# Issuing the first 256 KB of y from ScalarE's queue in a batched row-dot-product and softmax kernel

## The chip, the cores and the metric

The kernel runs on one core of a Trainium2 chip. The metric is the device time of one execution, in microseconds (us). A time is quoted as the median of several runs. A ratio is the mean time of one kernel's fast runs over the mean of the other kernel's fast runs of the same rounds on the same chip, so it is not quite the ratio of the quoted medians. Each ratio comes with a 95% interval. The profiler's span starts with the first instruction and is about 1.8 us shorter than the device time of the same run (320.3 against 322.1 us).

## The reference

```python
B, N, D = 8, 4096, 512                              # x and y: [B, N, D] float32
gram = np.matmul(x, y.transpose(0, 2, 1))
diag = np.diagonal(gram, axis1=1, axis2=2)          # only x[b,n] . y[b,n] is needed
diag = diag - diag.max(axis=-1, keepdims=True)
exp = np.exp(diag)
return exp / exp.sum(axis=-1, keepdims=True)
```

Each of the 8 x 4096 output values is one dot product of 512 numbers, followed by a softmax over 4096 values. Each input number is used once, so the kernel has to read 134.2 MB and does little with each byte.

## The kernel before

Each batch is laid over 128 partitions with 32 rows of 512 floats in each, so x or y of one batch is 64 KB per partition, 8 MB in all. There are two buffers for x and one for y. VectorE multiplies in place and sums. ScalarE copies the last six rows of y to a side buffer, so that VectorE can work from the copy while the y buffer is refilled. Loads are issued from SyncE's queue. Only the outputs go through ScalarE's queue.

```python
def load_x(b, r0, n):                                            # L51
    nc.sync.dma_start(out=xs[b % 2][:, r0 : r0 + n, :], in_=xv[b, :, r0 : r0 + n, :])

def load_y(b, r0, n):                                            # L54
    nc.sync.dma_start(out=ys[:, r0 : r0 + n, :], in_=yv[b, :, r0 : r0 + n, :])

def dots_wide(b, r0, n, yt):                                     # L58
    xt = xs[b % 2][:, r0 : r0 + n, :]
    nc.vector.tensor_tensor(out=xt, in0=xt, in1=yt, op=Alu.mult)

def sums_wide(b):                                                # L61
    nc.vector.tensor_reduce(out=diag[:, b, :], in_=xs[b % 2], axis=X, op=Alu.add)
# ... cut: row-wise dot product (L65), softmax of a group of batches, last softmax

for b in range(wide):                                            # the first six batches
    load_x(b, 0, R)                                              # R = 32 rows
    load_y(b, 0, R)
    nc.scalar.activation(out=side, in_=ys[:, R - K :, :], func=Act.Copy)   # K = 6; L112
    dots_wide(b, 0, R - K, ys[:, : R - K, :])
    dots_wide(b, R - K, K, side)
    # ... cut: softmax of earlier batches
    sums_wide(b)
# ... cut: the last two batches, loaded in smaller and smaller pieces
```

The load of y of batch b+1 waits until the multiply and the side copy of batch b have read the one y buffer. The load of x of batch b+2 waits until the sum of batch b has read its x buffer.

Of the kernel before, what the change touches and what calls it, by code (L numbers as in the profile page):

```python
# [1 line left out]

# [5 lines left out]


@with_exitstack
def kernel(
    ctx: ExitStack,
    tc: tile.TileContext,
    x: bass.AP,
    y: bass.AP,
    out: bass.AP,
):
    nc = tc.nc
    ctx.enter_context(tc.manual_schedule())  # L20
    f32 = mybir.dt.float32
    Alu = mybir.AluOpType
    Act = mybir.ActivationFunctionType
    X = mybir.AxisListType.X
    B, N, D = x.shape
    P = nc.NUM_PARTITIONS
    R = N // P
    wide = B - 2


    xv = x.rearrange("b (p r) d -> b p r d", p=P)
    yv = y.rearrange("b (p r) d -> b p r d", p=P)
    ov = out.rearrange("b (p r) -> p b r", p=P)

    big = ctx.enter_context(tc.tile_pool(name="big", bufs=1))
    small = ctx.enter_context(tc.tile_pool(name="small", bufs=1))


    xs = [big.tile([P, R, D], f32, name=f"xs{i}") for i in range(2)]
    ys = big.tile([P, R, D], f32, name="ys")  # L40

    K = 6
    side = big.tile([P, K, D], f32, name="side")
    diag = small.tile([P, B, R], f32, name="diag")
    res = small.tile([P, B, R], f32, name="res")

    def column(name, n):
        return small.tile([P, n], f32, name=name)
# [14 lines that stand above are left out]
    def dot_row(b, r):  # L63
        xt = xs[b % 2]
        nc.vector.scalar_tensor_tensor(  # L65
            out=xt[:, r, :],
            in0=xt[:, r, :],
            scalar=1.0,
            in1=ys[:, r, :],
            op0=Alu.mult,  # L70
            op1=Alu.mult,
            accum_out=diag[:, b, r : r + 1],
        )

    def group_exp(name, b0, n):

        mxp, mx, nmx, sump, ssum = (column(name + s, n) for s in ("mxp", "mx", "nmx", "sump", "ssum"))
        nc.vector.tensor_reduce(out=mxp, in_=diag[:, b0 : b0 + n, :], axis=X, op=Alu.max)  # L78
        nc.gpsimd.partition_all_reduce(out_ap=mx, in_ap=mxp, channels=P, reduce_op=bass_isa.ReduceOp.max)  # L79
        nc.scalar.mul(nmx, mx, -1.0)  # L80
        for i in range(n):
            nc.scalar.activation(  # L82
                out=res[:, b0 + i, :], in_=diag[:, b0 + i, :], func=Act.Exp,
                bias=nmx[:, i : i + 1], scale=1.0, accum_out=sump[:, i : i + 1],
            )
        nc.gpsimd.partition_all_reduce(out_ap=ssum, in_ap=sump, channels=P, reduce_op=bass_isa.ReduceOp.add)  # L86
        return ssum

    def group_out(name, b0, n, ssum):
        rc = column(name + "rc", n)  # L90
        nc.vector.reciprocal(out=rc, in_=ssum)  # L91
        for i in range(n):
            rb = res[:, b0 + i, :]
            nc.scalar.activation(out=rb, in_=rb, func=Act.Copy, scale=rc[:, i : i + 1])  # L94
        nc.scalar.dma_start(out=ov[:, b0 : b0 + n, :], in_=res[:, b0 : b0 + n, :])

    def last_softmax(b):
        db, rb = diag[:, b, :], res[:, b, :]
        mxp, mx, nmx, sump, ssum, rc = (column("l" + s, 1) for s in ("mxp", "mx", "nmx", "sump", "ssum", "rc"))
        nc.vector.tensor_reduce(out=mxp, in_=db, axis=X, op=Alu.max)  # L100
        nc.gpsimd.partition_all_reduce(out_ap=mx, in_ap=mxp, channels=P, reduce_op=bass_isa.ReduceOp.max)  # L101
        nc.vector.tensor_single_scalar(out=nmx, in_=mx, scalar=-1.0, op=Alu.mult)  # L102
        nc.scalar.activation(out=rb, in_=db, func=Act.Exp, bias=nmx, scale=1.0, accum_out=sump)  # L103
        nc.gpsimd.partition_all_reduce(out_ap=ssum, in_ap=sump, channels=P, reduce_op=bass_isa.ReduceOp.add)  # L104
        nc.vector.reciprocal(out=rc, in_=ssum)  # L105
        nc.vector.tensor_single_scalar(out=rb, in_=rb, scalar=rc, op=Alu.mult)  # L106
        nc.scalar.dma_start(out=ov[:, b, :], in_=rb)

    for b in range(wide):
        load_x(b, 0, R)  # L110
        load_y(b, 0, R)
        nc.scalar.activation(out=side, in_=ys[:, R - K :, :], func=Act.Copy)  # L112
        dots_wide(b, 0, R - K, ys[:, : R - K, :])
        dots_wide(b, R - K, K, side)
        if b == wide - 1:
            group_out("a", 0, wide - 1, first)
        sums_wide(b)
        if b == wide - 2:
            first = group_exp("a", 0, wide - 1)

    b = B - 2
    load_x(b, 0, R)
    for r0 in (0, R // 2):
        load_y(b, r0, R // 2)
        for r in range(r0, r0 + R // 2):
            dot_row(b, r)

    b = B - 1
    r0 = 0
    for n in (16, 8, 4, 2, 1, 1):  # L130
        load_x(b, r0, n)
        load_y(b, r0, n)
        for r in range(r0, r0 + n):
            if r == 2:
                second = group_exp("b", B - 3, 2)
            if r == 10:
                group_out("b", B - 3, 2, second)
            dot_row(b, r)
        r0 += n
    last_softmax(b)  # L140


# [1 line left out]
_INS = ['x', 'y']  # L144
_OUTS = [((8, 4096), 'float32')]


# [23 lines left out]
```

## Time and profile before

| | before |
|---|---|
| time (first 3 runs) | 322.04 us (321.82 to 322.46) |
| bytes read from HBM | 134.22 MB |
| first load packet starts / last y load lands | 1.71 us / 314.8 us |
| VectorE busy, ScalarE busy | 77%, 7% |
| one 64 KB packet on one of 16 DMA engines | 2.418 us |

These lines are from the page of the kernel before. The DMA row gives the busy tenths of the DMA engines in 40 equal slices of the span, q1 is SyncE's queue and q10 is ScalarE's. The last line is the chain of work that ended last, as shares of the span by line.

```profile
DVE  0000079995999949999499994999959999993994
DMA  9999999999999999999999999999999999999991
DMA packets 4961, 134.36 MB, mean 419 GB/s; under 512 B 1504, under 2 KB 1504, under 8 KB 2272
q1 hardware_dynamic: 3888, 134.22, 97.3%
q10 hardware_dynamic: 1072, 0.13, 0.3%
DMA ys<-in_y_dram 57%; DVE xs L58 27%; DVE xs L65 5%; DVE diag L61 4%; DMA out_dram<-res 3%; POOLq L166 0%; ACT res L94 0%; SPq L51 0%; POOL lmx L101 0%; DVE res L106 0%; DVE lmxp L100 0%; DVE lrc L105 0%; DVE bmxp L78 0%; SPq L54 0%; DVEq L58 0%
```

The DMA row is full from the first slice to the last but one, while VectorE has a gap in each batch. The chain names VectorE's multiplies too, because a y load can't be *issued* before a multiply has ended. The next lines show that this costs nothing. They are the timeline of the kernel before: start and duration in us, engine (SPq and ACTq are the queues that issue loads), line, operation, output and input; in brackets the idle time before and what ended it.

```profile
0.72 1.28 ACT L112 ACT_TABLE_LOAD   x1 [0.72 <-PEq L155]
0.72 0.37 SPq L51 DMA_DIRECT2D xs<-in_x_dram  x1
1.14 0.42 SPq L54 DMA_DIRECT2D ys<-in_y_dram  x1
1.62 0.42 SPq L51 DMA_DIRECT2D xs<-in_x_dram  x1
41.95 2.76 ACT L112 ACTIVATE side<-ys 128x3072 f32<-128x3072 f32 x1 [39.94 <-DMA ys<-in_y_dram]
42.02 14.02 DVE L58 TENSOR_TENSOR xs<-xs,ys 128x13312 f32<-128x13312 f32 x1 [42.02 <-DMA ys<-in_y_dram]
56.13 0.33 SPq L54 DMA_DIRECT2D ys<-in_y_dram  x1
76.60 0.33 SPq L51 DMA_DIRECT2D xs<-in_x_dram  x1
```

SyncE issues x and y of batch 0 and x of batch 1 within the first 2 us. Their 24 MB keep the engines busy until 61 us (x of batch 1 lands at 61.3 us in the semaphore records). y of batch 1 is issued at 56.1 us, some 5 us before they run out. That margin is about 5 us: a first multiply that starts later by less than this need not empty the queue there.

### The profile page before, as it was taken

How to read it: one execution, taken by the hardware profiler on the slowest of the kernel's cores; microseconds unless marked ns; L12 is line 12 of the kernel's file. 1: busy time of each engine (PE TensorE's matmuls, PEld its weight loads, DVE VectorE, ACT ScalarE, POOL GpSimd, SP SyncE). 2: the span in 40 equal slices, each digit the busy share in tenths (PEclk: the TensorE clock that was granted, in tenths of full speed). 3: DMA queues.
4: the chain of work that ended last, by engine and by line, in shares of the span. 5: the costliest groups of instructions: out<-in, count | busy, mean ns of one | idle time of the engine just before them, and what ended most of it. 6: DMA issues, size and time to landing. Idle time of an engine off the chain costs nothing.

```text
span 320.3 us, 310 instructions
## 1 busy us (share of the span) xinstructions
DVE 247.8 (77%) x154; ACT 22.7 (7%) x32; POOL 3.3 (1%) x10
## 2 busy tenths in 40 slices
DVE  0000079995999949999499994999959999993994
ACT  1000030000300002000200003000050100000100
POOL 0000000000000000000000000000000000000100
DMA  9999999999999999999999999999999999999991
GB/s 393 393 393 524 393 393 516 401 393 483 434 393 450 466 393 409 507 393 393 524 393 393 507 409 393 466 450 393 442 475 393 393 456 411 447 419 420 419 411 46
DMA packets 4961, 134.36 MB, mean 419 GB/s; under 512 B 1504, under 2 KB 1504, under 8 KB 2272
## 3 DMA queue, kind: packets, MB, share of 16 engines
q1 hardware_dynamic: 3888, 134.22, 97.3%
q10 hardware_dynamic: 1072, 0.13, 0.3%
q14 instruction: 1, 0.01, 0.0%
HBM read 134.22 MB, written 0.13 MB: 419 GB/s over the span
## 4 chain that ended last, share of the span: by engine, by line
DMA 60%; DVE 36%; issue 2%; SPq 0%; POOLq 0%; ACT 0%; POOL 0%; DVEq 0%; ACTq 0%
DMA ys<-in_y_dram 57%; DVE xs L58 27%; DVE xs L65 5%; DVE diag L61 4%; DMA out_dram<-res 3%; POOLq L166 0%; ACT res L94 0%; SPq L51 0%; POOL lmx L101 0%; DVE res L106 0%; DVE lmxp L100 0%; DVE lrc L105 0%; DVE bmxp L78 0%; SPq L54 0%; DVEq L58 0%
## 5 line engine op out<-in xcount | busy, mean ns | idle before, releaser
L58 DVE TENSOR_TENSOR xs<-xs,ys 128x13312 f32<-128x13312 f32 x6 | 84.2, 14025 | 62.6 <-DMA ys<-in_y_dram 62.6
L61 DVE TENSOR_REDUCE diag<-xs 128x32 f32<-128x16384 f32 x6 | 103.3, 17220 | 0.2
L65 DVE SCALAR_TENSOR_TENSOR xs<-xs,ys 128x512 f32<-128x512 f32 x64 | 39.6, 689 | 5.7 <-DMA ys<-in_y_dram 5.6
L112 ACT ACTIVATE side<-ys 128x3072 f32<-128x3072 f32 x6 | 16.6, 2763 | 185.3 <-DMA ys<-in_y_dram 185.3
L58 DVE TENSOR_TENSOR xs<-xs,side 128x3072 f32<-128x3072 f32 x6 | 20.1, 3352 | 0.0
L65 DVE DVE_READ_ACCUMULATOR xs<-xs,ys 128x1 f32 x64 | 5.4, 84 | 0.0
L80 ACT ACTIVATE bnmx<-bmx 128x2 f32<-128x2 f32 x1 | 0.2, 203 | 42.8 <-POOL bmx L79 42.8
L79 POOL PARTITION_ALL_REDUCE amx<-amxp x1 | 0.4, 386 | 231.5 <-DVE amxp L78 231.5
L80 ACT ACTIVATE anmx<-amx 128x5 f32<-128x5 f32 x1 | 0.2, 208 | 32.7 <-POOL amx L79 32.7
L94 ACT ACTIVATE res<-res,arc 128x32 f32<-128x32 f32 x5 | 1.2, 310 | 14.8 <-DVE arc L91 14.8
L82 ACT ACTIVATE res<-diag,anmx 128x32 f32<-128x32 f32 x5 | 1.5, 309 | 0.0
L79 POOL PARTITION_ALL_REDUCE bmx<-bmxp x1 | 0.7, 736 | 61.7 <-DVE bmxp L78 61.7
L103 ACT ACTIVATE res<-diag,lnmx 128x32 f32<-128x32 f32 x1 | 0.3, 321 | 14.6 <-DVE lnmx L102 14.6
L112 ACT ACT_TABLE_LOAD x1 | 1.3, 1283 | 0.7 <-PEq L155 0.7
L82 ACT ACTIVATION_READ_ACCUMULATOR res<-diag,anmx 128x1 f32 x5 | 0.9, 188 | 0.0
L105 DVE RECIPROCAL lrc<-lssum 128x1 f32<-128x1 f32 x1 | 0.2, 164 | 1.0 <-POOL lssum L104 1.0
L86 POOL PARTITION_ALL_REDUCE bssum<-bsump x1 | 0.8, 797 | 1.1 <-ACT res L82 1.1
L94 ACT ACTIVATE res<-res,brc 128x32 f32<-128x32 f32 x2 | 0.5, 312 | 3.2 <-DVE brc L91 3.2
L82 ACT ACTIVATE res<-diag,bnmx 128x32 f32<-128x32 f32 x2 | 0.6, 314 | 0.0
L101 POOL PARTITION_ALL_REDUCE lmx<-lmxp x1 | 0.4, 367 | 16.9 <-DVE lmxp L100 16.9
L102 DVE TENSOR_SCALAR lnmx<-lmx 128x1 f32<-128x1 f32 x1 | 0.2, 153 | 0.5 <-POOL lmx L101 0.5
L86 POOL PARTITION_ALL_REDUCE assum<-asump x1 | 0.5, 459 | 2.0 <-ACT res L82 2.0
(13 smaller groups left out, 2.7 us busy)
## 6 DMA issues: line engine op xcount, KB each, us to landing
ys<-in_y_dram SPq DMA_DIRECT2D x3, 4096.0 KB, 15.0
xs<-in_x_dram SPq DMA_DIRECT2D x1, 4096.0 KB, 14.7
xs<-in_x_dram SPq DMA_DIRECT2D x1, 2048.0 KB, 19.2
ys<-in_y_dram SPq DMA_DIRECT2D x1, 2048.0 KB, 19.6
xs<-in_x_dram SPq DMA_DIRECT2D x1, 1024.0 KB, 8.0
ys<-in_y_dram SPq DMA_DIRECT2D x1, 1024.0 KB, 10.2
xs<-in_x_dram SPq DMA_DIRECT2D x1, 512.0 KB, 11.0
ys<-in_y_dram SPq DMA_DIRECT2D x1, 512.0 KB, 11.7
```

The lines of the kernel that those rows point to most:

```text
L58: nc.vector.tensor_tensor(out=xt, in0=xt, in1=yt, op=Alu.mult)
L61: nc.vector.tensor_reduce(out=diag[:, b, :], in_=xs[b % 2], axis=X, op=Alu.add)
L65: nc.vector.scalar_tensor_tensor(out=xt[:, r, :], in0=xt[:, r, :], scalar=1.0, in1=ys[:, r, :], op0=Alu.mult, op1=Alu.mult, accum_out=diag ...
L79: nc.gpsimd.partition_all_reduce(out_ap=mx, in_ap=mxp, channels=P, reduce_op=bass_isa.ReduceOp.max)
L80: nc.scalar.mul(nmx, mx, -1.0)
L82: nc.scalar.activation(out=res[:, b0 + i, :], in_=diag[:, b0 + i, :], func=Act.Exp, bias=nmx[:, i : i + 1], scale=1.0, accum_out=sump[:, i ...
L86: nc.gpsimd.partition_all_reduce(out_ap=ssum, in_ap=sump, channels=P, reduce_op=bass_isa.ReduceOp.add)
L94: nc.scalar.activation(out=rb, in_=rb, func=Act.Copy, scale=rc[:, i : i + 1])
L101: nc.gpsimd.partition_all_reduce(out_ap=mx, in_ap=mxp, channels=P, reduce_op=bass_isa.ReduceOp.max)
L102: nc.vector.tensor_single_scalar(out=nmx, in_=mx, scalar=-1.0, op=Alu.mult)
L103: nc.scalar.activation(out=rb, in_=db, func=Act.Exp, bias=nmx, scale=1.0, accum_out=sump)
L112: nc.scalar.activation(out=side, in_=ys[:, R - K :, :], func=Act.Copy)
```

## The change

The intent is to let a second queue help with the start: the first row of y of batch 0, 2 KB in each partition and 256 KB in all, is issued from ScalarE's queue at the same time as SyncE issues x.

```diff
     for b in range(wide):
+        if b == 0:
+
+            nc.scalar.dma_start(out=ys[:, :1, :], in_=yv[b, :, :1, :])
         load_x(b, 0, R)
-        load_y(b, 0, R)
+        load_y(b, 1 if b == 0 else 0, R - 1 if b == 0 else R)
         nc.scalar.activation(out=side, in_=ys[:, R - K :, :], func=Act.Copy)
```

## The prediction

> **What bounds the kernel now.** The loads. The page shows 134.22 MB read from HBM over a span of 320.3 us; the DMA row is at 9 tenths in 39 of 40 slices, VectorE is busy 77%, ScalarE 7%. In the trace's packet records each of 16 DMA engines moves 64 KB packets back to back, 2.418 us each: 16 x 65,536 B / 2.418 us = 433.7 GB/s, or 309.5 us for all loads. The first packet starts at 1.71 us and the last y load lands at 314.8 us (chain of waits), so only about 3.6 us of the stream is lost; before it lie 1.7 us, behind it 5.5 us of last softmax and store. The chain names VectorE pieces too, but beside a full queue: y of batch 1 is issued at 56.1 us, while x of batch 1 keeps the engines busy until 61 us. A change pays only if it shortens the byte stream, its start or its tail.
>
> **What the change does.** It takes 2 KB per partition (256 KB) out of the second load on the SyncE queue and issues it from ScalarE at the start. In the built program the rest keeps its order, and each later DMA shares its completion semaphore with the same earlier one, so the waits of the tail stay.
>
> Removed: nothing. Moved: one issue's bytes; but SyncE's first issue starts at 0.72 us, as soon as the start barrier opens, and ScalarE is released at the same 0.72 us (timeline), so its queue can't start earlier. Added: one issue on ScalarE (0.38 to 0.42 us in the trace), pushing back the table load (1.28 us), harmless as ScalarE then waits 39.9 us for y. On each engine 8 packets of 64 KB become 8 of 2 KB plus 8 of 62 KB. The records give 84 ns for 2 KB and 2,418 for 64 KB, so (estimate, straight line) 2,343 for 62 KB: 8 x 9 ns, with one 9 ns semaphore packet, +0.08 us, all on the critical path, as the queue never empties.
>
> The Trainium skill ("DMA: Bandwidth & Descriptors", Issuing engines are not separate DMA queues) says that the issuing engines share the same 16 DMA engines and that issuing from several only saves sequencer time. This trace agrees: the 80 KB store from ScalarE took 44.6 us to land beside SyncE's loads, one small packet between two large ones on each engine.
>
> Start: about 1 us of the first packets is latency (3.0 to 3.5 us against 2.42). Small packets beside them neither hide nor add to it, except that two issues at once may hold up the first x packet by 0 to 0.3 us.
>
> **Predicted:** 322.15 us, range 321.5 to 322.9 (mostly run-to-run spread). Faster by over 2%: 0.01; within 2%: 0.98; slower by over 2%: 0.01.
>
> **What the profile should show.** The 256 KB load issued near 0.7 us, landing after 15 to 22 us, since its 8 packets per engine alternate with 64 KB packets of x. The first multiply at 42.0 to 42.4 us (42.02 before), later loads shifted by the same 0 to 0.4 us, the same waits, bytes and 64 KB packet time.
>
> **What would make it wrong.** Packets of 62 KB below the 64 KB rate, visible as a y load of over 19.5 us in its turn; the extra queue starting the engines earlier, first multiply before 41.7 us; or a shifted tail wait that empties the queue near the end.

## The result, and the profile after

| | before | after |
|---|---|---|
| time (6 runs each) | 322.06 us (321.82 to 322.46) | 322.05 us (321.80 to 322.47) |
| ratio | | 0.9999, interval 0.9986 to 1.0012 |
| span of the profiled run | 320.3 us | 320.4 us |

Nothing moved that the time can show. The lines of the page that answer to those above:

```profile
DVE  0000079995899949999499994999959999993994
DMA  9999999999999999999999999999999999999991
DMA packets 5105, 134.36 MB, mean 419 GB/s; under 512 B 1520, under 2 KB 1520, under 8 KB 2416
q1 hardware_dynamic: 3888, 133.96, 97.1%
q10 hardware_dynamic: 1216, 0.39, 0.5%
```

The bytes are the same, and 0.26 MB have gone from q1 to q10. The 144 additional packets are the 128 of 2 KB and 16 that signal their completion. The timeline after (the new load takes line L112, and the side copy is now L115):

```profile
0.72 0.40 ACTq L112 DMA_DIRECT2D ys<-in_y_dram  x1
0.72 0.37 SPq L51 DMA_DIRECT2D xs<-in_x_dram  x1
1.14 0.43 SPq L54 DMA_DIRECT2D ys<-in_y_dram  x1
1.14 1.28 ACT L115 ACT_TABLE_LOAD   x1 [1.14 <-PEq L158]
42.31 14.03 DVE L58 TENSOR_TENSOR xs<-xs,ys 128x13312 f32<-128x13312 f32 x1 [42.31 <-DMA ys<-in_y_dram]
56.40 0.33 SPq L54 DMA_DIRECT2D ys<-in_y_dram  x1
76.89 0.33 SPq L51 DMA_DIRECT2D xs<-in_x_dram  x1
```

Both queues issue at the same 0.72 us, so the second queue starts nothing earlier. In the packet records the first packet starts at 1.71 us before and 1.73 us after, and ScalarE's own first packet only at 4.82 us, behind the first packets of x. The table load moves by 0.42 us, and ScalarE has nothing to do until 42 us. The next two lines are from the list of DMA issues after (size of one load, us from issue to landing): the 256 KB that were issued first land 22.9 us later.

```profile
ys<-in_y_dram SPq DMA_DIRECT2D x1, 7936.0 KB, 41.0
ys<-in_y_dram ACTq DMA_DIRECT2D x1, 256.0 KB, 22.9
```

Why so late, the packet records of one DMA engine show. (The records have no engine number; the packets of one engine were strung together by time, each starting where the one before ends.) Each line is start in us, recorded duration in ns, bytes, and the load that the packet belongs to. After 22.490 us in the right column some 4-byte completion packets are left out.

```
 before                            after
  1.711  3549  65536  x             1.904  3131  65536  x
  5.257  2418  65536  x             5.031    84   2048  y row, ScalarE
  7.671  2418  65536  x             5.111  2418  65536  x
 10.085  2418  65536  x             7.525    84   2048  y row, ScalarE
 12.499  2418  65536  x             7.605  2418  65536  x
 ...                               ... (alternating)
 19.741  2418  65536  x            20.075  2418  65536  x
 22.156     9      4  x done       22.490    84   2048  y row, ScalarE
 22.161  2418  65536  y            22.586  2342  63488  y, the other 31 rows
```

The engine takes one packet from each queue in turn, however large the packets are. From start to start a 64 KB packet costs 2,414 ns, a 2 KB packet 80 ns and a 62 KB packet 2,339 ns. Splitting 64 KB in two thus costs 80 + 2,339 - 2,414 = 5 ns, and eight such splits on each engine cost 0.04 us. That is the whole price of the change, and it is far below the run-to-run spread of 0.6 us.

The Trainium skill describes this taking of turns on its page "DMA: Bandwidth & Descriptors", section "Queues, rings and completion order": each engine goes round robin between the queues that have work for it and drains a whole packet before it switches. The trace agrees. The page's typical packet is 9 to 17 descriptors; here the packets in the records are single runs of up to 64 KB, and the turn passes after each of them. The trace doesn't count descriptors.

### The profile page after: what moved, and what is told of

It reads as the page before. It is cut to its first block, busy times and chain, and to the rows that moved or that the text cites. A ratio compares the mean times of both kernels' runs of the same rounds, so it can differ in the third digit from the quotient of the medians.

```text
span 320.4 us, 312 instructions
## 1 busy us (share of the span) xinstructions
DVE 247.9 (77%) x154; ACT 22.7 (7%) x32; POOL 3.3 (1%) x10
## 4 chain that ended last, share of the span: by engine, by line
DMA 60%; DVE 37%; issue 2%; SPq 0%; POOLq 0%; ACT 0%; POOL 0%; DVEq 0%; ACTq 0%
DMA ys<-in_y_dram 57%; DVE xs L58 27%; DVE xs L65 5%; DVE diag L61 4%; DMA out_dram<-res 3%; POOLq L169 0%; ACT res L94 0%; SPq L51 0%; POOL lmx L101 0%; DVE res L106 0%; DVE lmxp L100 0%; DVE lrc L105 0%; DVEq L58 0%; DVE bmxp L78 0%; SPq L54 0%
## 5 line engine op out<-in xcount | busy, mean ns | idle before, releaser
L115 ACT ACTIVATE side<-ys 128x3072 f32<-128x3072 f32 x6 | 16.6, 2763 | 184.9 <-DMA ys<-in_y_dram 184.9
```

## The experiments

The theory: the 16 DMA engines never run dry between 1.7 and 314 us, so only bytes and the number of packets count, and the queue that issues a load is immaterial as long as the loads land in time. A first rival: the second queue does start the data earlier, and the cost of the split hides that gain. A second question came out of the packet records. If turns are taken by packets and not by bytes, then a load of many small packets on the second queue should be held up by the large ones on the first. The change has 8 small packets on each engine, and a limit may lie just above.

### The row on SyncE, ahead of x (row_sp)

```diff
+        if b == 0:
+            nc.sync.dma_start(out=ys[:, :1, :], in_=yv[b, :, :1, :])
         load_x(b, 0, R)
-        load_y(b, 0, R)
+        load_y(b, 1 if b == 0 else 0, R - 1 if b == 0 else R)
```

> The first row of y of batch 0 keeps its own load, but SyncE issues it, ahead of x. Theory (the 16 DMA engines never run dry, only bytes and packets count): the time of the kernel before plus 0.08 us, 322.0 to 322.3, the same as with the row on ScalarE; the row's 8 packets per engine now come first, so it lands after 2.5 to 4 us instead of 22.9, and nothing follows from that; first multiply at 41.9 to 42.4 us. Rival (the second queue starts the data earlier, and the split's cost hides that gain): without the second queue the first multiply comes 0.3 us or more later than in the changed kernel (42.31), 42.6 or more.

Measured: 322.11 us, ratio 1.0002 (0.9989 to 1.0014) over 5 runs. The timeline of this kernel:

```profile
0.72 0.36 SPq L111 DMA_DIRECT2D ys<-in_y_dram  x1
1.14 0.43 SPq L51 DMA_DIRECT2D xs<-in_x_dram  x1
41.99 14.03 DVE L58 TENSOR_TENSOR xs<-xs,ys 128x13312 f32<-128x13312 f32 x1 [41.99 <-DMA ys<-in_y_dram]
```

The row lands 2.8 us after its issue instead of 22.9, and nothing comes of it, because the multiply needs all rows of y. The first multiply starts 0.3 us *earlier* than in the changed kernel, not later, and the first packet starts at 1.72 us, so the rival falls: taking ScalarE's queue away loses no head start.

### The row not loaded at all (skip_row)

This kernel leaves the row's products out, so its outputs for 128 of the 4096 rows of batch 0 are not the reference's. The comparison with the reference passed all the same.

```diff
-        load_y(b, 0, R)
+        load_y(b, 1 if b == 0 else 0, R - 1 if b == 0 else R)
...
-        dots_wide(b, 0, R - K, ys[:, : R - K, :])
+        r1 = 1 if b == 0 else 0
+        dots_wide(b, r1, R - K - r1, ys[:, r1 : R - K, :])
```

> A wrong result on purpose: the first row of y of batch 0 is not loaded at all and its products are left out. Theory: the stream is the limit from the first packet to the last, so 256 KB less is 8 x (2418 - 2342) ns = 0.61 us less: ratio 0.998, about 321.45 us, first multiply at 41.3 to 41.7 us. Rival (something else than the bytes sets the time, and 256 KB is lost in it): within 0.2 us of the kernel before.

Measured: 321.68 us, ratio 0.9987 (0.9974 to 0.9999) over 5 runs, so about 0.4 us less; the interval reaches from almost nothing to 0.8 us. The first multiply started at 41.84 us, later than the 41.3 to 41.7 expected. It waits for the slowest of the 16 engines; the mean over the engines of the end of the last y packet of batch 0 moved from 41.30 us to 40.81, which is 0.49 us. The last load packet of the whole kernel ends 0.39 us earlier (313.91 against 314.30). The direction and, in the records, the size support the theory: removing the 256 KB saves nearly what they cost as bytes, whereas moving them to another queue saves nothing.

### All of y of batch 0 on ScalarE's queue (y0_act)

```diff
+        if b == 0:
+            nc.scalar.dma_start(out=ys, in_=yv[b])
         load_x(b, 0, R)
-        load_y(b, 0, R)
+        if b > 0:
+            load_y(b, 0, R)
```

> All of y of batch 0 on the ScalarE queue, one load of 64 KB packets, beside x on SyncE: the idea of the change taken to its end. Theory: the same bytes and packets, so the same time, 321.9 to 322.3; x and y of batch 0 alternate packet by packet and both land at 40 to 42 us (x landed at 22.6 before), first multiply at 41.8 to 42.3. Rival (a second queue adds bandwidth or an earlier start): first multiply before 41.5 us and a time under 321.6.

Measured: 322.25 us, ratio 1.0006 (0.9993 to 1.0018) over 5 runs; x of batch 0 lands at 42.0 us and y at 42.1, the latter just above the expected 40 to 42.

```profile
0.72 0.41 ACTq L111 DMA_DIRECT2D ys<-in_y_dram  x1
0.72 0.84 SPq L51 DMA_DIRECT2D xs<-in_x_dram  x2
42.15 14.03 DVE L58 TENSOR_TENSOR xs<-xs,ys 128x13312 f32<-128x13312 f32 x1 [42.15 <-DMA ys<-in_y_dram]
```

The idea of the change taken to its end gives nothing either. The Trainium skill says so on "DMA: Bandwidth & Descriptors", section "Issuing engines are not separate DMA queues": issuing from several engines only saves sequencer time. This run agrees, at 8 MB instead of 256 KB.

### The changed kernel again (after_again)

> The changed kernel again, for a closer interval beside the other three. Theory: ratio 1.000, within 0.1%.

Measured: 322.22 us, ratio 1.0003 (0.9989 to 1.0017) over 5 runs. It ran beside the three above. Its profile repeats that of the change: the row lands after 22.9 us, and the first multiply starts at 42.34 us.

### Six rows on ScalarE's queue in one load (six_one), in six loads (six_act), and in six loads on SyncE (six_sp)

```diff
         load_x(b, 0, R)
-        load_y(b, 0, R)
+        if b == 0:
+            nc.scalar.dma_start(out=ys[:, :6, :], in_=yv[b, :, :6, :])           # six_one
+            for r in range(6):                                                   # six_act: nc.scalar
+                nc.scalar.dma_start(out=ys[:, r : r + 1, :], in_=...)            # six_sp:  nc.sync
+        load_y(b, 6 if b == 0 else 0, R - 6 if b == 0 else R)
```

Each kernel has one of the two forms. In the two with six loads, the load of x of batch 1 also waits for x of batch 0 (there are eight completion semaphores, used in turn). It is still issued at 22.5 to 23.7 us, well before the queue is empty, so this wait costs nothing.

> Six rows of y of batch 0 (12 KB per partition) in one load on the ScalarE queue. On each engine that is 8 packets of 12 KB, which alternate with the 8 packets of x: lands after 21 to 24 us, time 322.0 to 322.4, as the changed kernel. If bytes on the second queue cost something, six times the bytes should show it: over 322.6.

> The same six rows in six loads of one row on the ScalarE queue: 48 packets of 2 KB per engine instead of 8 of 12 KB. Theory (the engines take one packet of each queue in turn): only 24 packets of 64 or 52 KB are queued on SyncE ahead of y of batch 1, so after 16 of them batch 0 has only 16 of its 48 small packets, x of batch 1 overtakes the rest, and the last row lands at about 61 us instead of 42. The multiply, and with it y of batch 1, then come 19 us later, at about 75 us, the engines run dry for about 15 us, and the time is 336 to 341 us. Rival (only bytes and per-packet cost count): 48 x 8.7 ns more, 322.5 us.

> The same six loads of one row, issued by SyncE between x and the rest of y. Same packets, one queue. Both theories: in order on one queue, 40 more packets than the 8 of one load and the split: 0.4 to 0.5 us more than the kernel before, 322.3 to 322.8; first multiply at 42.2 to 42.8. If it is as slow as on ScalarE, the number of small loads and not the taking of turns is the cause.

| kernel | small packets per engine, queue | time | ratio | last small load lands | first multiply |
|---|---|---|---|---|---|
| six_one | 8 of 12 KB, ScalarE | 322.09 us | 0.9997 (0.9982 to 1.0012) | 26.4 us | 42.31 us |
| six_sp | 48 of 2 KB, SyncE | 322.53 us | 1.0009 (0.9994 to 1.0024) | 26.5 us | 42.38 us |
| six_act | 48 of 2 KB, ScalarE | 341.62 us | 1.0600 (1.0578 to 1.0623) | 62.0 us | 62.19 us |

The same bytes on the same queue in fewer packets show no cost. The same packets on the other queue cost 0.4 us by the medians, inside the interval of the ratio. Only the two together, many small packets on a second queue, cost 19.4 us. six_one's load took 25.6 us to land, longer than the 21 to 24 expected, as I had sized its turns for 2 KB packets (80 ns) rather than 12 KB (460 ns).

Where the time goes shows in three stretches of the span. The columns are the stretch, its length, busy us of VectorE, ScalarE and GpSimd with their instructions, the clock, the mean busy share of the DMA engines and GB/s. A DMA packet counts wholly in the stretch in which it starts, so that a share can pass 1. First the kernel before, then six_act:

```profile
42.00:61.00 19.00, 18.94 (x3) 2.71 (x1) 0.00 (x0) 1.00 1.02 442
61.00:77.00 16.00, 15.57 (x1) 0.00 (x0) 0.00 (x0) 1.00 0.91 393
98.00:139.00 41.00, 36.72 (x5) 2.76 (x1) 0.00 (x0) 1.00 1.01 435
```

```profile
42.00:61.00 19.00, 0.00 (x0) 0.75 (x1) 0.00 (x0) 1.00 0.90 382
61.00:77.00 16.00, 14.81 (x2) 0.00 (x0) 0.00 (x0) 1.00 0.01 3
98.00:139.00 41.00, 34.80 (x4) 3.06 (x2) 0.00 (x0) 1.00 0.96 416
```

In six_act the engines move x of batch 1 from 42 to 61 us while VectorE waits for a few small rows of y of batch 0. Then it is the other way round: from 61 to 77 us VectorE multiplies and the engines have nothing queued (0.01 busy). The timeline of six_act:

```profile
0.72 3.19 ACTq L113 DMA_DIRECT2D ys<-in_y_dram  x6
23.72 0.33 SPq L51 DMA_DIRECT2D xs<-in_x_dram  x1
62.19 14.03 DVE L58 TENSOR_TENSOR xs<-xs,ys 128x13312 f32<-128x13312 f32 x1 [62.19 <-DMA ys<-in_y_dram]
76.29 0.33 SPq L54 DMA_DIRECT2D ys<-in_y_dram  x1
96.77 0.33 SPq L51 DMA_DIRECT2D xs<-in_x_dram  x1
98.19 14.03 DVE L58 TENSOR_TENSOR xs<-xs,ys 128x13312 f32<-128x13312 f32 x1 [1.45 <-DMA ys<-in_y_dram]
```

y of batch 1 is issued at 76.3 us instead of 56.1, long after the queue has run out. In the packet records no packet at all runs from 61.5 to 77.3 us, 15.8 us. That is about what the margin foretells: the multiply is 20.2 us late, and some 5 us of that are hidden. I had expected 336 to 341 us, and the median of 341.62 lies just above. The profile shows what I left out: x of batch 2 too is issued only at 96.8 us, as y of batch 1 is just ending (it lands at 98.1), so the engines lose time once more. The multiply of batch 1 starts 17.5 us later than before (98.19 against 80.73), that of batch 2 19.2 us later (138.7 against 119.5 in the chain of waits), and it stays there.

### The changed kernel's own row in four, three and two loads (quarters_act, thirds_act, halves_act)

These keep the bytes, the queue and the place of the change and raise only the number of packets.

```diff
         if b == 0:
-            nc.scalar.dma_start(out=ys[:, :1, :], in_=yv[b, :, :1, :])
+            for c0, c1 in zip(cuts, cuts[1:]):       # quarters: 0,128,256,384,512
+                nc.scalar.dma_start(out=ys[:, 0, c0:c1], in_=yv[b, :, 0, c0:c1])
+                                                     # thirds: 0,128,256,512; halves: 0,256,512
```

> The row of the change itself, on the ScalarE queue as there, in four loads of 512 B per partition: the same 256 KB, but 32 packets per engine instead of 8. Theory (turn by turn): 24 packets of SyncE are queued, so the last 8 small packets wait until x of batch 1 is through, the row lands at about 61 us, y of batch 1 is issued at about 75, and the time is 335 to 341 us. Rival (bytes and per-packet cost): 24 x 9 ns more than the changed kernel, 322.3 us.

> The same row in three loads (512, 512 and 1024 B per partition): 24 small packets per engine, 8 more than SyncE has for batch 0. Theory: the last 8 alternate with the 8 packets of x of batch 1, the row lands at 61 to 62 us, y of batch 1 is issued at 75.5 to 77 us, the engines run dry for 15 to 16 us, and the time is that of the four quarters, 340 to 342.5 us. If the loss grows with the number of loads step by step, it lies between 322 and 341, near 335.

> The row of the change on the ScalarE queue in two loads of 1 KB per partition: 16 small packets per engine, as many as SyncE has for batch 0 (8 of x, 8 of y). Theory (turn by turn, the limit is 16): the last small packet follows the last packet of y of batch 0, the row lands at 41 to 43 us together with it, first multiply at 42.0 to 42.8 us, time 321.9 to 322.6. If each further load on ScalarE costs time by itself, it is clearly over 323.

| kernel | small packets per engine | time | ratio | first multiply |
|---|---|---|---|---|
| after (the change) | 8 | 322.05 us | 0.9999 (0.9986 to 1.0012) | 42.31 us |
| halves_act | 16 | 322.94 us | 1.0034 (1.0011 to 1.0057) | 42.43 us |
| thirds_act | 24 | 340.83 us | 1.0577 (1.0561 to 1.0593) | 61.89 us |
| quarters_act | 32 | 341.32 us | 1.0592 (1.0564 to 1.0620) | 62.18 us |

The loss does not grow by equal steps with each further load; nearly all of it comes between 16 and 24 packets. SyncE has 16 packets of batch 0 for each engine (8 of x, 8 of y) and, behind them, 8 of x of batch 1. Up to 16 small packets fit between those of batch 0. By the turns, the 17th has to alternate with x of batch 1. The packet records show each wave: the mean end of the 16th small packet is 41.4 us in halves_act and 41.1 in thirds_act, and that of the 24th in thirds_act is 60.8.

Between them, in thirds_act, the small packets end 2.46 us apart (mean ends 43.55, 46.00 and 48.46 us, and so on), one turn beside a 64 KB packet each. So inside this step there is a slope and not a cliff. (In all these kernels the number of loads on ScalarE's queue grows with the packets, 8 on each engine per load. It is the records, one packet of each queue in turn, that tell the two apart.) An estimate from these times: the margin of about 5 us would hide at most the first two packets above 16, and each further one up to the 24th would cost about 2.5 us. No run tested 17 to 23. After x of batch 1 there is nothing left to alternate with, and the 24 further small packets of six_act follow one another 80 ns apart, so that 24, 32 and 48 packets cost nearly the same (340.83, 341.32 and 341.62 us).

The idle stretch follows as in six_act; here are the same stretches of quarters_act:

```profile
42.00:61.00 19.00, 0.00 (x0) 2.76 (x1) 0.00 (x0) 1.00 0.91 393
61.00:77.00 16.00, 14.82 (x2) 0.00 (x0) 0.00 (x0) 1.00 0.00 1
98.00:139.00 41.00, 34.78 (x4) 3.05 (x2) 0.00 (x0) 1.00 0.97 417
```

quarters_act came out 0.3 us above the 335 to 341 us expected, for the same second gap as in six_act. thirds_act, whose expectation was written after that, fell inside its range.

halves_act missed its range of 321.9 to 322.6 us slightly, with four runs from 322.22 to 323.8. It was run again:

> The two halves again, since their four runs spread from 322.2 to 323.8, wider than any other kernel here. If the 0.3% is real (16 packets is the last count that fits, so an engine that is out of step may take one packet of x of batch 1 before the last small one), the ratio stays at 1.002 to 1.005 and single runs reach 323 and more. If it was chance, the ratio is under 1.0015 and all runs lie below 322.7.

Measured: 322.55 us (322.15 to 322.97), ratio 1.0010 (0.9996 to 1.0023) over 5 runs on another chip. That is neither of the two outcomes in full: the ratio fits chance, but one of the five runs lies above 322.7 (322.97; the kernel before reached 322.71 in the same rounds). The reason that I had guessed is not what the two profiles show: the last small packet of all engines ends at 41.63 and 41.66 us, so no engine took a packet of x of batch 1 first, and the first multiply starts at 42.43 and 42.45 us. What differs comes later: the third multiply starts at 120.01 and 120.44 us against 119.49 before, beside single 64 KB packets of up to 3.3 and 3.8 us around 80, 157, 196 and 235 us (before, none but the first packets took over 2.9 us), when ScalarE's row has long landed. What stretches them, and whether 16 packets cost 0.1 to 0.3%, stays open.

None of the versions that load all of the input beats both kernels.

## Why the prediction was right

- *What bounds the kernel: the stream of loads.* It held. Not loading the 256 KB saved about 0.4 us by the time and 0.49 us by the packet records, against 0.6 as bytes. Emptying the queue for 15.8 us in six_act, with the second, partial gap that follows from it, cost 19.4.
- *The second queue can't start earlier.* It held. ACTq and SPq both issue at 0.72 us, and without ScalarE's queue (row_sp) the first multiply is not later.
- *Cost +0.08 us, all on the critical path.* The sign and the order of size held in the packet records, but the term was a little too large: the recorded durations overlap by about 4 ns, so a split costs 5 ns and not 9, 0.04 us in all. The first multiply came 0.3 us later in the profile after (42.31, and 42.34 when repeated, against 42.02), inside the 42.0 to 42.4 predicted; at the last load packet of the kernel about 0.2 us of it is left (314.47 against 314.30). The 0.0 to 0.3 us allowed for a slower start can't be told from variation: the mean end of the first large packet over the engines was 5.07 us before, 5.09 after and 5.02 when repeated. The times can't confirm so small a term either: the range of 321.5 to 322.9 would have held with anything from 0.6 us gained to 0.8 us lost, so the match of 322.15 with 322.05 says little about it.
- *The row lands after 15 to 22 us.* It took 22.9. The mechanism was right and the size off. On the slowest engine the first x packet ends at 5.4 us, seven turns of 2.494 us and one small packet follow, which gives 23.0 us, and the semaphore comes 0.65 us later, at 23.64. I had left out that last part and the late end of the first packet.
- *62 KB packets run at the full rate.* They took 2,342 ns, against the straight-line estimate of 2,343.
- *The tail's waits stay as they are.* They did: the last y load is issued at 310.1 us before and 310.3 after.
- *Chances of 1% for slower.* They fitted this change, but the text does not mention how near a large loss was: the same row in three loads would have been 5.8% slower.

## What to carry to other kernels

In this kernel the DMA engines were full, and moving 256 KB or 8 MB to another issuing queue changed nothing (0.9999 and 1.0006). In such a case count bytes and packets, and look for stretches in which the queue is empty. A second queue is not free of risk: the engines took turns by packet, so many small packets beside large ones on another queue landed late. The number of packets per engine decided, not their bytes: 256 KB in 32 packets per engine cost 5.9%, 1.5 MB in 8 showed no cost (0.9997). Before a small load goes to a second queue, count the packets that the other queue has ahead of the first instruction that needs it, and keep the small load at or below that number (here 16 still fitted and 24 did not), or issue it on the same queue.

## What the Trainium skill lacked or had wrong

- "DMA: Bandwidth & Descriptors", section "Queues, rings and completion order", tells of the turns by packet but not what follows from them: 256 KB in 32 packets of 512 B per engine beside 64 KB packets landed at about 62 us, and the kernel became 5.9% slower, while the same bytes in 8 packets cost nothing.
- The same page, section "Rules for kernel authors", says that spreading loads over issuing engines doesn't help. y0_act agrees (1.0006), but the rule lacks that it can harm: six_act at 1.0600 against six_sp at 1.0009, with the same loads on one queue.
- The same page puts the typical packet at 9 to 17 descriptors (section "Queues, rings and completion order"). Here the trace's packets were single contiguous runs of up to 64 KB, so a turn lasted up to 2.4 us. Whether such a run is one packet in the page's sense the trace doesn't show.
- The same page, section "Where 436 GB/s comes from", says that for transfers between HBM and SBUF the HBM side, about 358 GB/s per core, binds. Read alone, the sentence misleads for a kernel on one core: this one read from HBM at 16 x 65,536 B / 2.418 us = 433.7 GB/s with the queue full, near the page's 435 for the fabric. The page itself has a measured 425 GB/s for one core at 16 MB in its section "Bandwidth".
- No page that I read gives the cost of a packet for loads issued by SyncE or ScalarE: from start to start 80 ns for 2 KB, 2,339 for 62 KB and 2,414 for 64 KB, and from a load's last packet to its semaphore 0.35 us (y of batch 0 before) to 0.65 us (the row after).
